# Keys copied and norm products made behind a filling step, attention's filling in a fixed period, and a gate block's weight sums made one block earlier, in a hybrid attention and recurrence block

## The chip, the cores and the metric

The kernel runs on one core of a Trainium2 chip. The engines are TensorE (PE: matmuls, PEld: its weight loads), VectorE (DVE), ScalarE (ACT), GpSimd (POOL) and SyncE (SP), whose queue issues most loads. The metric is the time of one execution on the device in microseconds, as the median of several runs. The profile is of one further execution, recorded by the hardware profiler.

## The reference

One layer works on 1024 tokens of width 1024 in float32: a normalisation, one wide input projection, two branches in parallel, gates that merge them, an output projection, and an MLP with a squared ReLU. Cut to what the change touches:

```python
u = rmsnorm(x, norm1_g) @ w_in          # q, k, v of attention; f, i, q, g of the recurrence; two gates
# attention, 8 heads of 64: weights by a running product over the keys
w = where(mask, exp(log_beta + between), 0);  o_sb = w @ v
# HGRN2, 4 heads of 128: S_t = diag(f_t) S_{t-1} + k_t v_t^T, o_t = S_t^T q_t
o_hg = hgrn2_chunkwise(silu(q_hg), k_hg, i_hg, log_f)
o_hg = rmsnorm(o_hg, hg_norm_g) * silu(g_hg)
merged = sigmoid(gate_sb + b0) * (o_sb @ w_o_sb) + sigmoid(gate_hg + b1) * (o_hg @ w_o_hg)
h = x + merged @ w_out
```

Every product in float32 is made of three matmuls on a high and a low half of both operands (`three`), so each operand is first split: a copy on ACT makes the high half (L157), a subtraction on DVE the low half (L162). Large projections (gates, output, MLP) use sums of blocks in place of some products, so that weights and inputs are also added before they are split.

## The kernel before

**What sets the order.** The program is written as one list of instructions, and a planner that runs when the kernel is built gives each engine its own order: by what it estimates to be ready, and among ready ones the instruction written first. It also deals out tiles. `slot` gives one of 40 full tiles of 128 x 1024, `half` and `slot_n` (up to 512 columns) one of 10 half tiles, `bank` one of 8 PSUM banks, and weights on their way use two buffers each of `raw`, `whi` and `wlo`; a tile that isn't free is waited for. On the chip each engine then follows its own order and waits at semaphores. Where the author wants an order, `after(ins, earlier)` puts one instruction behind another on the same engine; `load` (L136) chains all loads on SP in the order in which they are written.

**Filling.** PE's order has two lanes. "main" blocks are those with a chain of work on other engines between them: scores and turned weights of attention, levels and tails of the recurrence. "fill" blocks are projections, which need nothing of that chain. `Stream` (L504) holds the filling as a list of jobs, each a generator; `st.advance(n, upto)` takes n steps of it, but not past job `upto`. A step of a projection is six matmuls of 512 columns. A projection job has nine steps: the fifth also evicts the first half, the ninth has no matmul and only evicts the second. The first step of a job also splits the weights of the next and starts the load of the one after (`prefetch`).

**Attention** (L2610 to L2648). 64 items, eight blocks of 128 queries for each of eight heads, in the order 7, 0, 6, 1, 5, 2, 4, 3. Item i writes the running product of item i+1 (`weights`, a scan on DVE), the scores of item i+2 (`scores`), its share of filling steps, then the turn of its own weights by PE with their split (`turn`: tiles wTh and wTl), then the value product (`values`: tile po) of the last pair of blocks that is complete. So values run behind blocks 1, 5 and 3 and, in the middle of its turn, behind block 7. The shares of filling come from `n_fill`, spread evenly over the 64 items.

**The recurrence** (L2651 to L2671). For each of four heads `hg_levels` has a first part and seven levels. Level l > 0 copies the keys that it needs into a half tile (`scores_of`, L1096 to L1099, ACT, tile ksl), multiplies them with the queries on PE (tile sl), lays the scores into place, then multiplies keys, queries and decays on DVE for the next level. `hg_tail` of the head before turns keys, sums states, and makes the output: matmuls into two banks (pho), squares with their sums on ACT (hon), a root on POOL (`inv_rms`, L266 and L270), the product of bank and root on DVE (L1281, into hon), and two rounds later transposes. After each `yield` of the one or the other, the loop takes `FILL[h]` filling steps on average (2.0 to 3.4).

**The gate blocks** (`GatePair` and `gates`, L1767 to L1983). Ten blocks, the first two of them (8 and 9) for the branch's own gate, the third is block 0. `load` fetches three blocks of weights and, for the others than 8 and 9, the output weights; `load_sums` fetches partial results; `split` adds weight blocks three times and splits what comes out; then follow products x6, y5, x7, y3 into two banks, gX and gY. In `gates`, while block v is made, `next_pair` splits block n, the one behind it, and loads block m, the one behind that. The first block is loaded and split earlier, in `sum_forms` (L1562), which runs beside the filling and whose last parts run just before `gates`. `held` are gate products whose last steps wait for this stage; they fill in between.

## Time and profile before

| | |
|---|---|
| median of 3 runs | 1428.94 us (1428.68 to 1429.35) |
| profiled execution | 1427.22 us |
| its span, first to last instruction | 1425.4 us |
| mean granted TensorE clock | 0.998 |
| busy share: PE, DVE, ACT, POOL | 99%, 75%, 47%, 12% |

The profiled execution's own time is 1.8 us above its span and 1.7 us below the median. In rows of the order of time the columns are: start in us from the span's start, duration in us, engine, line of the kernel, operation, output<-inputs, shapes, count, and in brackets the engine's idle time before it and what ended it. Names leave out numbers of buffers, so that ksl is the copy of the keys of any head and level. Rows of waits are: who waited, for whom, total us, how often, longest. A line such as L129 is that of a helper; the tiles tell which part of the kernel it is.

### The profile page before, as it was taken

To read this page: it belongs to the slowest core of one execution; us is meant where nothing else is said; L and a number is where in the kernel's file an instruction comes from. 1 tells how busy PE (TensorE), PEld (TensorE's weight loads), DVE (VectorE), ACT (ScalarE), POOL (GpSimd) and SP (SyncE) were. 2 spreads that over 40 slices of the span, in tenths; PEclk is the share of its full clock that TensorE was granted. 3 is DMA by queue.
4 is the path that set the end of the run, shared out by engine and by line. 5 is a ranking of instruction groups with operands and counts; after the bars stand their busy time and mean duration, and the time that the engine had idled before them with its cause. 6 is when DMAs were issued, how large, how long until landed. Compare 5 with 4: busy or idle time off the path is not lost.

```text
span 1425.4 us, 18660 instructions
## 1 busy us (share of the span) xinstructions
PE 1406.0 (99%) x6824; PEld 1179.2 (83%) x6824; DVE 1066.6 (75%) x1463; ACT 668.1 (47%) x1147; POOL 166.4 (12%) x318
## 2 busy tenths in 40 slices
PE   9999999999999999999999999999999999999997
PEld 8888888888887888788888888888888888888886
DVE  6688887778478858897788897677666657768765
ACT  6455556554245446433334764445444443433343
POOL 3023433310001111000000300000000000000042
PEclk9999999999999999999999999999999999999999
DMA  8256977954213676464485515444446974776724
GB/s 252 82 141 200 173 157 170 228 127 123 87 52 104 207 228 230 162 214 155 153 290 207 185 39 183 162 158 138 142 146 236 356 264 152 275 280 237 277 98 172
DMA packets 169556, 258.18 MB, mean 181 GB/s; under 512 B 31404, under 2 KB 92376, under 8 KB 169432
## 3 DMA queue, kind: packets, MB, share of 16 engines
q1 hardware_dynamic: 148280, 196.15, 40.9%
q0 software_dynamic: 16320, 50.34, 13.8%
q10 hardware_dynamic: 4864, 10.49, 2.1%
q8 instruction: 54, 0.88, 0.3%
q14 instruction: 38, 0.31, 0.1%
HBM read 186.69 MB, written 84.94 MB: 191 GB/s over the span
## 4 chain that ended last, share of the span: by engine, by line
PE 91%; DVE 4%; ACT 2%; DMA 1%; issue 1%; POOL 0%; SPq 0%; ACTq 0%; POOLq 0%; DVEq 0%
PE pm L129 21%; PE pX L129 9%; PE pW L129 6%; PE pY L129 6%; PE pjqk L129 6%; PE gY L129 3%; PE pji L129 3%; PE pga L129 3%; PE pyh L129 3%; PE gX L129 3%; PE pjq L129 3%; PE pjf L129 3%; PE po L129 3%; PE pwX L129 2%; PE pjv L129 2%; PE z L129 2%
## 5 line engine op out<-in xcount | busy, mean ns | idle before, releaser
L859 DVE TENSOR_TENSOR_SCAN rm<-rm,bits 128x512 f32<-128x512 f32 (+6 forms) x72 | 87.6, 1222 | 26.7 <-ACT rm L840 24.3
L157 ACT CAST whid<-w 128x1024 fp32r<-128x1024 f32 x30 | 31.6, 1054 | 154.3 <-PE pm L129 86.9
L129 PE MATMUL pm<-wlod,sh 128*128 128x512 f32 x240 | 93.5, 390 | 0.0
L129 PE MATMUL pm<-whid,sh 128*128 128x512 f32 x240 | 93.4, 389 | 0.0
L129 PE MATMUL pm<-whid,sl 128*128 128x512 f32 x240 | 93.4, 389 | 0.0
L129 PE MATMUL pm<-tl,sh 128*128 128x512 f32 (+1 forms) x210 | 81.3, 387 | 0.0
L129 PE MATMUL pm<-th,sl 128*128 128x512 f32 (+1 forms) x210 | 81.3, 387 | 0.0
L129 PE MATMUL pm<-th,sh 128*128 128x512 f32 (+1 forms) x210 | 81.3, 387 | 0.0
L162 DVE TENSOR_TENSOR wlod<-w,whid 128x1024 fp32r<-128x1024 f32 x30 | 36.6, 1221 | 55.1 <-ACT whid L157 55.0
L157 ACT CAST wTh<-pw 128x128 fp32r<-128x128 f32 (+3 forms) x96 | 43.8, 481 | 56.3 <-PE pw L132 51.6
L2387 POOL TENSOR_SCALAR fss<-fss 128x1 f32<-128x1 f32 x8 | 4.5, 561 | 562.0 <-ACT fsc L2382 561.5
L162 DVE TENSOR_TENSOR sl<-sa,sh 128x1024 fp32r<-128x1024 f32 x56 | 68.2, 1218 | 0.4 <-ACT sh L157 0.4
L162 DVE TENSOR_TENSOR wTl<-pw,wTh 128x512 fp32r<-128x512 f32 (+2 forms) x96 | 50.4, 546 | 22.5 <-ACT wTh L157 21.0
L157 ACT CAST sh<-sa 128x1024 fp32r<-128x1024 f32 x56 | 57.2, 1046 | 8.2 <-DMA sa<-ad 8.2
L129 PEld LDWEIGHTS pm<-wlod,sh 128*128 128x128 f32 x240 | 45.0, 188 | 9.8 <-DVE wlod L162 0.4
L129 PEld LDWEIGHTS pm<-whid,sh 128*128 128x128 f32 x240 | 45.1, 188 | 9.3
L129 PEld LDWEIGHTS pm<-whid,sl 128*128 128x128 f32 x240 | 45.0, 188 | 9.4
L129 PE MATMUL pX<-sqh,t1l 128*128 128x512 f32 x128 | 49.9, 390 | 0.0
L129 PE MATMUL pX<-sql,t1h 128*128 128x512 f32 x128 | 49.9, 390 | 0.0
L129 PE MATMUL pX<-sqh,t1h 128*128 128x512 f32 x128 | 49.8, 389 | 0.0
L129 PEld LDWEIGHTS pm<-tl,sh 128*128 128x128 f32 x210 | 39.5, 188 | 8.1
L129 PEld LDWEIGHTS pm<-th,sl 128*128 128x128 f32 x210 | 39.5, 188 | 8.0
(985 smaller groups left out, 4414.8 us busy)
## 6 DMA issues: line engine op xcount, KB each, us to landing
w<-in_w_ff_dram SPq DMA_DIRECT2D x72, 512.0 KB, 5.7
sa<-ad SPq DMA_DIRECT2D x52, 512.0 KB, 6.7
tg<-in_w_in_dram POOLq DMA_DIRECT2D x16, 512.0 KB, 9.5
ad<-a SPq DMA_DIRECT2D x32, 256.0 KB, 4.5
ad<-s SPq DMA_DIRECT2D x16, 512.0 KB, 3.3
tw<-in_w_out_dram POOLq DMA_DIRECT2D x24, 256.0 KB, 5.8
pr<-pd SPq DMA_DIRECT2D x10, 512.0 KB
x<-in_x_dram SPq DMA_DIRECT2D x8, 512.0 KB, 10.5
```

What stands on the lines that cost most here:

```text
L129: return pe(nc.tensor.matmul(*a, **k))
L157: hi_last[0] = after(in_turn("act", nc.scalar.copy(dst, src)), hi_behind[0])
L162: nc.vector.tensor_tensor(out=dst, in0=src, in1=hi.bitcast(F32), op=ALU.subtract),
L859: sc = nc.vector.tensor_tensor_scan(out=rr, data0=rr, data1=bits[:, 1024 - nk + a : 1024 - nk + b][:, ::-1], initial=rm[:, b : b + 1] if i ...
L2387: nc.gpsimd.tensor_scalar(out=ssq, in0=ssq, scalar1=1.0 / D, scalar2=EPS, op0=ALU.mult, op1=ALU.add)
```

## The change

- `keys_of` is split off `scores_of`. Level l puts the copy of level l+1's keys into a list, `soon`, and the loop of the recurrence now takes its filling steps one by one and empties the list after each. So the copy is written behind the first filling step of level l instead of behind all of them.
- The product of bank and root in `hg_tail` goes into the same list.
- In attention `n_fill` is 116 instead of 111 and the share 14 steps for each head of eight items, always 1, 2, 2, 2, 1, 2, 2, 2 (before, the pattern shifted from head to head); filling may run into the job behind, q of head 2.
- The third gate block's weights are loaded in the last part of `sum_forms`, into two full tiles of their own, and its three adds (`sums`) stand where its load was, in the first block's `next_pair`. Its `split` leaves them out.

```diff
+    soon = []
+
     def hg_levels(h):
...
+        ahead = {}
+
+        def keys_of(name, H):
+            ahead[name] = slot_n(f"k{name}", 512)
+            nc.scalar.copy(
+                ahead[name].rearrange("p (n s h) -> p s n h", s=2, h=H), crossed(k, 0, H)
+            )
+
         def scores_of(name, H):
-            keys = slot_n(f"k{name}", 512)
-            nc.scalar.copy(
-                keys.rearrange("p (n s h) -> p s n h", s=2, h=H), crossed(k, 0, H)
-            )
+            keys = ahead.pop(name)
             open_block("main")
...
             hg_level[0] = mul(right, right, left)
+            if l < 6:
+                soon.append(lambda l=l, H=H: keys_of(f"sl{h}_{l + 1}", 2 * H))
...
             rstd = inv_rms(ssq, 4, 1.0 / P, f"hn{h}_{half}")
-            mul(chunks(on), chunks(po), rstd.unsqueeze(2).to_broadcast([P, 4, P]))
+            soon.append(
+                lambda on=on, po=po, rstd=rstd: mul(
+                    chunks(on), chunks(po), rstd.unsqueeze(2).to_broadcast([P, 4, P])
+                )
+            )
...
             if i == 3:
                 gates_in[0].load_sums()
                 gates_in[0].split()
+            if i == 7:
+                gates_in[2].load()
             yield
...
-                if self is gates_in[0]
+                if self in (gates_in[0], gates_in[2])
...
+        def sums(self):
+            r0, r1 = self.raw
+            s0, s1 = slice(0, 512), slice(512, 1024)
+            add(r0[:, s0], r0[:, s1], r0[:, s0])
+            add(r1[:, s0], r1[:, s1], r0[:, s0])
+            add(r0[:, s1], r1[:, s1], r0[:, s1])
...
-            after(add(r0[:, s0], r0[:, s1], r0[:, s0]), first)
-            add(r1[:, s0], r1[:, s1], r0[:, s0])
+            if self is not gates_in[2]:
+                after(add(r0[:, s0], r0[:, s1], r0[:, s0]), first)
+                add(r1[:, s0], r1[:, s1], r0[:, s0])
...
-            add(r0[:, s1], r1[:, s1], r0[:, s1])
+            if self is not gates_in[2]:
+                add(r0[:, s1], r1[:, s1], r0[:, s1])
...
-        if m:
+        if m is gates_in[2]:
+            m.sums()
+        elif m:
             m.load()
...
-    n_fill = 9 * (NHS - 1 + 5) + 3
     n_first = 4
+    n_fill = n_first + 14 * NHS
...
-        st.advance(want - done, j_att)
+        st.advance(want - done, j_q[2])
...
-                    st.advance(int(owed), upto)
+                    for step in range(int(owed)):
+                        st.advance(1, upto)
+                        while soon:
+                            soon.pop(0)()
                     owed -= int(owed)
```

## The prediction

> **What bounds the kernel.** I read the page first, then busy time by stretches, then the waits of the matmul engine, then the order of time around each of its waits.

> ```profile
> PE 1406.0 (99%) x6824; PEld 1179.2 (83%) x6824; DVE 1066.6 (75%) x1463; ACT 668.1 (47%) x1147; POOL 166.4 (12%) x318
> ```

> TensorE (PE) is busy for 1406.0 us, 99% of the span. The change adds and removes no matmul, so it can only win PE's idle time, and only where it reaches. The next view has one row per stage: projections (to 85), attention (to 318), the gated recurrence with its filling (to 560), the first gate blocks (to 600), the rest.

> ```profile
> core 0: us, PE busy (x) PEld busy (x) DVE busy (x) ACT busy (x) POOL busy (x), PEclk, DMA share, GB/s
> 0.00:85.00 85.00, 82.03 (x419) 69.56 (x420) 55.75 (x115) 45.04 (x91) 17.02 (x40) 1.00 0.56 166
> 85.00:318.00 233.00, 230.18 (x1331) 198.89 (x1330) 188.41 (x238) 134.25 (x308) 74.38 (x156) 1.00 0.76 172
> 318.00:560.00 242.00, 237.84 (x1258) 201.59 (x1258) 176.84 (x306) 109.57 (x239) 25.73 (x42) 1.00 0.44 144
> 560.00:600.00 40.00, 38.49 (x170) 31.58 (x169) 33.98 (x47) 18.14 (x24) 2.59 (x5) 1.00 0.61 205
> 600.00:1110.00 510.00, 510.00 (x2294) 423.26 (x2293) 395.79 (x537) 238.64 (x339) 22.47 (x43) 1.00 0.50 172
> ```

> PE idles 2.82 us in attention, 4.16 in the recurrence, 1.51 in the first gate blocks, and not at all from 600 to 1110. The sum, 8.5 us, is all that lies in the change's reach. Who ends these waits, from 85 to 600:

> ```profile
> PE sl L129 <- ACT ksl L1097: 3.6, 3, 2.0
> PE po L129 <- DVE wTl L162: 2.7, 4, 1.0
> PE gY L129 <- DVE pr L1324: 1.5, 1, 1.5
> PE pga L129 <- DVE wga7wlo L162: 0.5, 1, 0.5
> PE po L129 <- ACT wTh L157: 0.2, 1, 0.2
> ```

> Ten waits, each with a part of the change aimed at it: level scores (sl) wait for the copy of the keys (ksl, `keys_of`), the attention's value products (po) for the low half of the turned weights (wTl), gate block gY for a subtraction, a filling step for the low half of its weights.

> A wait costs slightly more than its idle time, since the modelled ends of matmuls overlap the next start:

> ```profile
> 209.55 0.40 PE L129 MATMUL pjqk<-xnh,wqk6h 128*128 128x512 f32 x1
> 209.78 0.40 PE L129 MATMUL pjqk<-xnl,wqk6h 128*128 128x512 f32 x1
> 211.02 0.39 PE L129 MATMUL po<-wTl,V 128*128 128x256 f32 x1 [0.84 <-DVE wTl L162]
> ```

> Starts stand 0.23 us apart where nothing waits, and 1.24 here: 1.01 lost for 0.84 idle. I add these 0.17 us to each wait. The prices are then: keys 3.56 + 3 x 0.17 = 4.1 us; attention 2.82 + 5 x 0.17 = 3.7; gY 1.7; wga7wlo 0.7. Together 10.2 us.

> **The keys' copies.** Before, the copy of level l+1 is written behind all filling steps of level l; after, behind the first one. The same 24 copies run; none is added.

> ```profile
> 514.98 0.69 ACT L1290 ACTIVATE on<-pot,prm 128x512 f32<-128x512 f32 x1 [3.39 <-PE pot L132]
> 516.38 0.69 ACT L1460 ACTIVATE g<-pga,prm 128x512 f32<-128x512 f32 x1 [0.71 <-PE pga L129]
> 516.96 0.61 ACT L1097 COPY ksl<-k 128x512 f32<-128x512 f32 x1
> ```

> ```profile
> 510.65 0.69 DVE L170 TENSOR_TENSOR k<-k,pp 128x512 f32<-128x512 f32 x1
> ```

> ```profile
> 515.94 0.40 PE L129 MATMUL pga<-xnh,wga1wlo 128*128 128x512 f32 x1
> 517.62 0.38 PE L129 MATMUL sl<-q,ksl 128*128 128x128 f32 x1 [1.28 <-ACT ksl L1097]
> ```

> The keys are final at 510.65 + 0.69 = 511.34, and ACT then stands idle for 3.39 us; yet the copy comes last, behind two evictions that wait for PE, the second being of the filling step written just ahead of it. Copied where they are ready, the keys would be there at 512, and PE would go on at 516.2. The largest wait, 1.96 us at 448.88, has the same form; its product and its copy:

> ```profile
> 439.48 0.68 DVE L170 TENSOR_TENSOR k<-k,pp 128x512 f32<-128x512 f32 x1
> ```

> ```profile
> 448.20 0.62 ACT L1097 COPY ksl<-k 128x512 f32<-128x512 f32 x1
> ```

> What is late next is the queries' product, which VectorE (DVE) does right behind the keys' and as fast (0.7 us), in both places well before PE asks. So I take the whole 4.1 us. Bounds: 0 (the copies keep their place in ACT's order, which the build's planner sets) and 4.1; the loss is a rival below. A copied tile lives longer by one or two filling steps and takes one of ten half tiles; I price that among the new waits.

> ```profile
> L1097 ACT COPY ksl<-k x24: 607/622/698, 324.5 to 529.0; 128x512 f32<-128x512 f32 x24
> ...
> DVE k L170: 20.9, 8
> ```

> ACT already waits in front of key copies, 20.9 us in 8 waits, and what stands behind them waits too: a queue in its written order. [...]

> **The norm products.** Eight products (hon) move behind the first filling step after their squares.

> ```profile
> 551.67 0.69 DVE L170 TENSOR_TENSOR hon<-pho,hn_y 128x512 f32<-128x512 f32 x1 [1.18 <-POOL hn_y L270]
> 552.27 0.68 DVE L162 TENSOR_TENSOR wga7wlo<-wga7r,wga7whi 128x512 fp32r<-128x512 f32 x1
> ```

> This one waits 1.18 us for POOL's root, the low half of wga7 stands behind it, and PE waits for that (0.7 us). Put behind, the product would let wga7wlo go first. Whether it does is the planner's estimate of POOL against ACT, which no row shows: between 0 and 0.7, I take half, 0.35. The other seven hide beside PE's work; their readers, the transposes, come two filling rounds later. The norm's bank stays open for one filling step more.

> **The attention.** Filling rises from 111 to 116 steps, and each head gets the same 1, 2, 2, 2, 1, 2, 2, 2 over its eight blocks (7, 0, 6, 1, 5, 2, 4, 3). A step of six matmuls is 1.36 us (six starts 0.23 apart); five more of them here are five fewer later, so they cost nothing as such. I counted both lists: before, every wait above 0.5 us falls on a value product right behind a block in which a job ends and the next starts, or one without a matmul of filling. One of them on DVE:

> ```profile
> 164.83 1.20 DVE L1522 TENSOR_TENSOR xs<-xs,xnl 128x1024 f32<-128x1024 f32 x1
> 166.06 0.70 DVE L162 TENSOR_TENSOR KS<-pjqk,KS 64x512 fp32r<-64x512 f32 x1
> 166.77 0.68 DVE L162 TENSOR_TENSOR QL<-pjqk,QH 64x512 fp32r<-64x512 f32 x1
> 167.38 1.21 DVE L162 TENSOR_TENSOR wqk5l<-wqk5r,wqk5h 128x1024 fp32r<-128x1024 f32 x1
> 168.51 0.68 DVE L162 TENSOR_TENSOR wTl<-pw,wTh 128x512 fp32r<-128x512 f32 x1
> ```

> The job's end (KS, QL), the next weights (wqk5l) and an input sum stand ahead of wTl, 3.8 us. In the new list this bundle sits right ahead of a value product in two places: head 2, block 4 (the same bundle, one block earlier, but with 12 matmuls of filling behind it instead of 6: I take 0.9) and head 7, block 6 (no input sums left: 0.1). Head 1, block 7 keeps one step behind a job's end: 0.4. The block without filling moves to head 4, block 7, where its value product follows 3 us later, enough for 1.4 us of copy and subtraction: 0. Small ones 0.3. So 1.7 us come back and 2.0 are won; bounds 3.7 won and, with the single step now ahead of the values in all seven later heads and 1.0 for each, 7.0 - 3.7 = 3.3 lost.

> **The gate block.** The third block's three adds move from 577 to 586 into the first block's time, its four loads ahead of the held gates' loads on SP's queue.

> ```profile
> 576.50 0.69 DVE L1324 TENSOR_TENSOR gu<-gY,gu 128x512 f32<-128x512 f32 x1 [1.44 <-PE gY L129]
> ...
> 586.00 0.68 DVE L1321 TENSOR_TENSOR wg0r<-wg0r,wg0r 128x512 f32<-128x512 f32 x1
> ...
> 589.47 0.68 DVE L1324 TENSOR_TENSOR pr<-gY,pr 128x512 f32<-128x512 f32 x1
> ```

> PE waits until 590.21 for that last subtraction; its matmul before started at 588.31, so it could have gone on at 588.54. The row of 576.50 is the last with idle time; from there DVE's rows follow without a gap, with the three adds (577.71, 584.26, 586.00) among them. An add holds DVE for 0.6 us (from 586.00 to the next start at 586.60), so without them the subtraction ends 1.8 us earlier, at 588.36, and the wait goes, by 0.2 us. I take 1.7, bounds 0 and 1.7. The adds' new place is the stretch from 565 to 574, in which DVE has most of its idle 6.0 us of the row 560 to 600; if their loads land later, DVE stands before the adds, and bounds for that are 0 and those 6.0 us; I take 0. On SP's queue the loads now pass those of the held gates:

> ```profile
> 558.00 0.96 SPq L137 DMA_DIRECT2D y<-yd  x2
> ```

> ```profile
> 577.11 0.68 DVE L170 TENSOR_TENSOR g<-g,y 128x512 f32<-128x512 f32 x1
> ```

> Their reader comes 19 us later, which covers four more issues and a wait for the two further full tiles that the third block's weights now take from the pool.

> **New waits and the sum.** Earlier copies, later products and a filling that runs one step ahead reorder every engine from 90 to 600. Ten waits of 1.0 us on average stand there now; I take two new ones, 2.0 us (bounds 0 and 6). Sum: -4.1 - 0.35 - 2.0 - 1.7 + 2.0 = -6.1 us. The profiled execution took 1427.22 us, 1.7 below the median of the runs, 1428.94; the same 6.1 us off each gives 1421.1 and, for the median, **1422.8 us**.

> **Rivals.** (a) *The attention's waits only move.* For: a single step now precedes values in every head, and blocks in which a job ends still drift. Against: the three largest of before had the bundle ahead of them. Without the 2.0 us: 1424.8. (b) *The copies and products stay where they were*, as the planner sends what it deems ready: the change doesn't do what it says. For: in heads 0 and 1 ACT already waits for k, so copies run as early as they can there. Against: at 511 an idle ACT did not take a copy that was ready. Without 4.1 and 0.35, and with one new wait: -2.0 - 1.7 + 1.0 = -2.7, 1426.2. (c) *Slower: copies ahead of evictions.* In heads 2 and 3, twelve copies now stand before evictions of the filling. If one waits for its keys the mean of the 8 waits, 20.9 / 8 = 2.6 us, and PE needs the bank behind it, PE stands. Four such add 10.4 us: -6.1 + 10.4 = +4.3, 1433.2; from four on it is slower than before by more than a measurement can tell. Against: none of the 8 held PE.

> **Chances.** Forecast 0.47, (a) 0.20, (b) 0.18, (c) 0.12, and 0.03 that all ten waits go (1428.94 - 10.2 = 1418.7). A measurement of this kernel can tell about 0.2%, 2.9 us. The forecast is faster but for 0.04, (a) in three of four, (b) in two of five: faster 0.68, same 0.19, slower 0.13. The range 1419.5 to 1428.5 holds the forecast, (a) and (b), and leaves out (c) and the last case.

> **What would show it.** Right: no idle row at sl behind ksl from 430 to 520, with copies within 1 us of their k product; hon behind wga7wlo; gY without a wait and wg0r adds near 570; the largest remaining po wait in head 2. Wrong: copies still behind evictions (b); pga, pys or p evictions waiting behind ksl (c); po waits in most heads at block 7 (a); DVE idle before wg0r.

## The result and the profile after

| | median of runs (lowest to highest) | ratio to before, 95% interval |
|---|---|---|
| before | 1429.14 us (1428.68 to 1430.27) | |
| after | 1420.33 us (1418.52 to 1421.75) | 0.9936 [0.9919, 0.9954] |
| before, second set | 1428.26 us (1426.94 to 1428.96) | |
| after, second set | 1420.94 us (1418.93 to 1421.28) | 0.9948 [0.9936, 0.9961] |

The change wins 8.8 us in the first set and 7.3 in the second, against 6.1 forecast. The profiled execution of after took 1421.75 us, with a span of 1420.0 (before: 1427.22 and 1425.4). Busy time by stretches, first three columns PE, PEld and DVE as before:

```profile
core 0: us, PE busy (x) PEld busy (x) DVE busy (x) ACT busy (x) POOL busy (x), PEclk, DMA share, GB/s
85.00:318.00 233.00, 230.01 (x1315) 198.88 (x1314) 185.32 (x234) 130.52 (x300) 74.86 (x159) 0.99 0.76 172
318.00:560.00 242.00, 241.97 (x1291) 206.50 (x1290) 182.45 (x314) 116.33 (x249) 26.25 (x42) 1.00 0.46 149
560.00:600.00 40.00, 40.00 (x179) 33.10 (x178) 36.66 (x52) 16.81 (x22) 2.17 (x4) 1.00 0.54 176
```

PE's idle time in the recurrence fell from 4.16 us to 0.03 and in the first gate blocks from 1.51 to nothing. In attention it did not fall at all: 2.82 before, 2.99 after. And the PEclk column, which was 1.00 in every row of before, is 0.99 there. PE's waits of after, from 85 to 600:

```profile
PE po L129 <- DVE wTl L162: 2.3, 2, 2.2
PE pjq L129 <- ACT osb L934: 0.4, 1, 0.4
PE z L129 <- ACT rm L840: 0.2, 1, 0.2
```

All ten old waits are gone; nearly all that is left is one wait of 2.17 us. It ends at 171.18, at head 2, block 3, with DVE as the engine that is late:

```profile
165.62 1.22 DVE L1535 TENSOR_TENSOR xs<-xs,xnl 128x1024 f32<-128x1024 f32 x1
166.75 1.22 DVE L859 TENSOR_TENSOR_SCAN rm<-rm,bits 128x512 f32<-128x512 f32 x1
168.00 0.70 DVE L162 TENSOR_TENSOR KS<-pjqk,KS 64x512 fp32r<-64x512 f32 x1
168.72 0.68 DVE L162 TENSOR_TENSOR QL<-pjqk,QH 64x512 fp32r<-64x512 f32 x1
169.32 1.21 DVE L162 TENSOR_TENSOR wqk5l<-wqk5r,wqk5h 128x1024 fp32r<-128x1024 f32 x1
170.46 0.87 DVE L162 TENSOR_TENSOR wTl<-pw,wTh 128x512 fp32r<-128x512 f32 x2
```

```profile
168.07 0.60 PE L132 MATMUL pw<-ident,rm 128*128 128x128 f32 x4
168.42 0.36 PE L129 MATMUL po<-wTh,V 128*128 128x256 f32 x1
168.62 0.40 PE L129 MATMUL pjq<-xnh,wq0h 128*128 128x512 f32 x1
171.18 0.39 PE L129 MATMUL po<-wTl,V 128*128 128x256 f32 x1 [2.17 <-DVE wTl L162]
...
171.64 0.28 PE L129 MATMUL po<-wTh,V 128*128 128x256 f32 x1
171.76 0.31 PE L129 MATMUL po<-wTl,V 128*128 128x256 f32 x1
171.88 0.40 PE L129 MATMUL po<-wTh,V 128*128 128x256 f32 x1
172.09 0.42 PE L129 MATMUL po<-wTl,V 128*128 128x256 f32 x1
172.30 0.41 PE L129 MATMUL po<-wTh,V 128*128 128x256 f32 x1
```

DVE has no gap from 165.62 to wTl. Behind the wait the value products start 0.12 us apart up to 171.88, and from there 0.21 apart: PE's clock has halved. The stretches around it, in after:

```profile
168.47:171.88 3.41, 1.24 (x9) 0.92 (x8) 3.40 (x6) 0.59 (x1) 0.79 (x2) 1.00 0.83 136
171.88:175.30 3.42, 3.42 (x14) 3.13 (x13) 2.69 (x4) 1.64 (x4) 1.36 (x2) 0.50 0.81 190
175.30:178.71 3.41, 3.41 (x25) 3.09 (x25) 2.66 (x2) 1.65 (x6) 0.19 (x2) 1.00 0.89 185
```

The granted clock is 0.50 for 3.41 us, then full again. Half of 3.41, so by estimate 1.7 us, is lost behind the wait, and no idle row shows it.

**Does it add up?** I took each matmul's distance from the start of the one before, subtracted the usual (median) distance of matmuls of its kind, and added up all excess over 0.06 us from 85 to 620. That is 21.6 us before and 16.0 after; the difference, 5.6, is the difference of the two spans (5.4). In attention the excess rose from 9.8 to 11.0; behind it, it fell from 11.7 to 5.0.

### The profile page after: what moved, and what is told of

It reads as the page before. It is cut to its first block, busy times and chain, and to the rows that moved or that the text cites. A ratio compares the mean times of both kernels' runs of the same rounds, so it can differ in the third digit from the quotient of the medians.

```text
span 1420.0 us, 18679 instructions
## 1 busy us (share of the span) xinstructions
PE 1406.0 (99%) x6824; PEld 1181.1 (83%) x6824; DVE 1066.9 (75%) x1463; ACT 667.8 (47%) x1147; POOL 164.4 (12%) x318
## 4 chain that ended last, share of the span: by engine, by line
PE 95%; DVE 1%; ACT 1%; DMA 1%; issue 1%; SPq 0%; POOL 0%; POOLq 0%; DVEq 0%
PE pm L129 21%; PE pX L129 9%; PE pW L129 6%; PE pY L129 6%; PE pjqk L129 5%; PE gY L129 4%; PE gX L129 4%; PE pga L129 4%; PE pjf L129 3%; PE pji L129 3%; PE pyh L129 3%; PE pjq L129 3%; PE pys L129 3%; PE po L129 3%; PE pwX L129 2%; PE z L129 2%
## 5 line engine op out<-in xcount | busy, mean ns | idle before, releaser
L157 ACT CAST whid<-w 128x1024 fp32r<-128x1024 f32 x30 | 31.6, 1054 | 154.1 <-PE pm L129 83.2
L129 PE MATMUL pm<-whid,sh 128*128 128x512 f32 x240 | 93.4, 389 | 0.0
L129 PE MATMUL pm<-wlod,sh 128*128 128x512 f32 x240 | 93.4, 389 | 0.0
L129 PE MATMUL pm<-whid,sl 128*128 128x512 f32 x240 | 93.4, 389 | 0.0
L129 PE MATMUL pm<-tl,sh 128*128 128x512 f32 (+1 forms) x210 | 81.3, 387 | 0.0
L129 PE MATMUL pm<-th,sl 128*128 128x512 f32 (+1 forms) x210 | 81.3, 387 | 0.0
L129 PE MATMUL pm<-th,sh 128*128 128x512 f32 (+1 forms) x210 | 81.3, 387 | 0.0
L162 DVE TENSOR_TENSOR wlod<-w,whid 128x1024 fp32r<-128x1024 f32 x30 | 36.7, 1223 | 53.6 <-ACT whid L157 53.6
L157 ACT CAST wTh<-pw 128x512 fp32r<-128x512 f32 (+2 forms) x96 | 43.8, 483 | 57.9 <-PE pw L132 54.2
L162 DVE TENSOR_TENSOR sl<-sa,sh 128x1024 fp32r<-128x1024 f32 x56 | 68.3, 1219 | 0.4 <-ACT sh L157 0.3
L162 DVE TENSOR_TENSOR wTl<-pw,wTh 128x512 fp32r<-128x512 f32 (+2 forms) x96 | 50.4, 546 | 21.8 <-ACT wTh L157 20.7
L157 ACT CAST sh<-sa 128x1024 fp32r<-128x1024 f32 x56 | 57.2, 1046 | 9.0 <-DMA sa<-ad 9.0
L129 PEld LDWEIGHTS pm<-wlod,sh 128*128 128x128 f32 x240 | 45.1, 188 | 9.5
L129 PEld LDWEIGHTS pm<-whid,sl 128*128 128x128 f32 x240 | 45.1, 188 | 9.3
L129 PEld LDWEIGHTS pm<-whid,sh 128*128 128x128 f32 x240 | 45.0, 187 | 9.4
L129 PE MATMUL pX<-sqh,t1l 128*128 128x512 f32 x128 | 49.9, 390 | 0.0
L129 PE MATMUL pX<-sql,t1h 128*128 128x512 f32 x128 | 49.9, 390 | 0.0
L129 PE MATMUL pX<-sqh,t1h 128*128 128x512 f32 x128 | 49.8, 389 | 0.0
L840 ACT ACTIVATE rm<-z 128x512 f32<-128x512 f32 (+3 forms) x96 | 44.5, 501 | 8.4 <-DMA sx<-xs 5.7
L129 PEld LDWEIGHTS pm<-th,sh 128*128 128x128 f32 x210 | 39.5, 188 | 8.1
```

Of the source, the lines that this page charges most:

```text
L129: return pe(nc.tensor.matmul(*a, **k))
L157: hi_last[0] = after(in_turn("act", nc.scalar.copy(dst, src)), hi_behind[0])
L162: nc.vector.tensor_tensor(out=dst, in0=src, in1=hi.bitcast(F32), op=ALU.subtract),
L840: scored[0] = nc.scalar.activation(rm[:, s0 : s0 + m], z[:, :m], AF.Sigmoid, scale=-0.125)
```

## The experiments

My theory was that each part removes the waits it is aimed at, and that they add. The rival was that the whole filling, moved by one step, did the recurrence's share too. Every part was first made alone in the kernel before; the median of before beside these four was 1427.71 us.

**The keys' copies alone.**

```diff
-            keys = slot_n(f"k{name}", 512)      # in scores_of
-            nc.scalar.copy(...)
+            keys = ahead.pop(name)
...
+            if l < 6:
+                soon.append(lambda l=l, H=H: keys_of(f"sl{h}_{l + 1}", 2 * H))
```

> Before with the keys' copies alone moved behind the first filling step. Theory 1 (each part removes its own waits): the three waits of sl for ksl between 430 and 520 us are gone, 4.1 us less (about 1425.0), all other waits of before stand unchanged. Theory 2 (the waits went because the filling runs one step further ahead in the recurrence): at least two of the three waits are still there, the time within 1 us of before. Theory 3 (early copies hold back evictions behind them): the waits for ksl are gone but new ones for evictions stand in their place, the gain under 2 us.

1422.22 us, ratio 0.996 [0.9947, 0.9972]: 5.5 us less than the median of before. The three waits for ksl are gone, every other wait of before is still there:

```profile
PE po L129 <- DVE wTl L162: 2.6, 4, 1.0
PE gY L129 <- DVE pr L1333: 1.5, 1, 1.5
PE pga L129 <- DVE wga7wlo L162: 0.5, 1, 0.5
PE po L129 <- ACT wTh L157: 0.2, 1, 0.2
```

The copy for the scores that waited at 517.62, with what follows it on ACT, and the scores on PE:

```profile
508.11 0.62 ACT L1101 COPY ksl<-k 128x512 f32<-128x512 f32 x1
511.59 0.69 ACT L1299 ACTIVATE on<-pot,prm 128x512 f32<-128x512 f32 x1 [2.86 <-PE pot L132]
512.98 0.69 ACT L1469 ACTIVATE g<-pga,prm 128x512 f32<-128x512 f32 x1 [0.70 <-PE pga L129]
```

```profile
512.55 0.39 PE L129 MATMUL pga<-xnh,wga1wlo 128*128 128x512 f32 x1
512.78 1.05 PE L129 MATMUL sl<-q,ksl 128*128 128x128 f32 x8
```

It now stands ahead of the two evictions that held it, is done at 508.73, and the scores start 0.23 us behind the matmul before them. Theory 1 holds; the gain is somewhat above the 4.1 that idle time and restart give. By the excess of starts it is 5.0 from 270 to 560: after each wait the second matmul was 0.1 us late too, and a delay of 0.3 us at wga0wlo (483.29) went as well. The 0.5 us above that come from before: 12 of its 27 executions have a mean granted clock of 0.997 and took 1428.86 us on average, the other 15, at 0.998 or 0.999, took 1427.26. Against these 15 the five of this kernel (0.998 or 0.999, mean 1422.20) gain 5.1. The last section says where the two groups come from.

**The norm products alone.**

```diff
-            mul(chunks(on), chunks(po), rstd...)
+            soon.append(lambda on=on, po=po, rstd=rstd: mul(chunks(on), chunks(po), rstd...))
```

> Before with the eight norm products alone moved behind the first filling step after their squares. Theory 1: the low half of wga7 goes ahead of the product that waits for POOL's root, PE's wait of 0.5 us near 553 is gone, 0.7 us less (about 1428.4). Theory 2: that wait stands or another takes its place, no change. The difference is at the edge of what the timing can tell; the trace decides.

1427.35 us, ratio 0.9999 [0.999, 1.0008]: nothing. (Its eight executions at 0.998 or 0.999 took 1427.24 us on average, those of before 1427.26.) On DVE the product is still ahead of the low half of wga7 and still waits for POOL:

```profile
551.89 0.69 DVE L170 TENSOR_TENSOR hon<-pho,hn_y 128x512 f32<-128x512 f32 x1 [1.18 <-POOL hn_y L270]
552.50 0.68 DVE L162 TENSOR_TENSOR wga7wlo<-wga7r,wga7whi 128x512 fp32r<-128x512 f32 x1
```

Written later, it kept its place. Why the planner put it there, the trace does not show.

**The attention's filling alone.**

```diff
-    n_fill = 9 * (NHS - 1 + 5) + 3
     n_first = 4
+    n_fill = n_first + 14 * NHS
...
-        st.advance(want - done, j_att)
+        st.advance(want - done, j_q[2])
```

> Before with the attention's fixed filling period alone (116 instead of 111 steps). Theory 1: the five waits of po of before go (3.7 us) and the waits seen after the whole change stand here too, the largest, some 2.2 us, near 171 at head 2, block 3; a net gain between 0 and 1.5 us, less by up to 1.7 us where PE's granted clock halves behind that wait. The three waits for ksl in the recurrence are still there, moved or not. Theory 2: with the filling one step ahead, the waits for ksl near 449, 462 and 517 are gone without any change to the copies, and the gain is over 4 us.

1426.75 us, ratio 0.9991 [0.9982, 1.0]. PE's waits:

```profile
PE sl L129 <- ACT ksl L1097: 4.0, 4, 1.5
PE po L129 <- DVE wTl L162: 2.3, 2, 2.2
PE gY L129 <- DVE pr L1324: 1.1, 1, 1.1
PE pjq L129 <- ACT osb L934: 0.2, 1, 0.2
```

The waits for ksl are now four, and with 4.0 us in sum no shorter than the three of before (3.6): the rival, theory 2, falls. The five attention waits are gone and the 2.17 us wait stands in their place. The wait for wga7wlo is gone here, with the norm products where they were: it was this part that removed it.

**The gate block's sums alone.**

```diff
+            if i == 7:
+                gates_in[2].load()
...
-        if m:
+        if m is gates_in[2]:
+            m.sums()
+        elif m:
             m.load()
```

> Before with the third gate block's loads and sums alone moved into the first gate block. Theory 1: the wait of gY for the subtraction (1.5 us near 590) is gone and the sums stand between 560 and 580, 1.7 us less (about 1427.2). Theory 2: DVE stands before the sums for their loads and PE waits for something else there: gain under 0.5 us.

1426.6 us, ratio 0.9989 [0.9981, 0.9998]: 1.1 us less. The second and third sum wait 0.30 us for their load and hold up nobody; gY does not wait any more.

```profile
572.55 1.29 DVE L1321 TENSOR_TENSOR wg0r<-wg0r,wg0r 128x512 f32<-128x512 f32 x2 [0.30 <-DMA wg0r<-in_w_in_dram]
```

This profiled execution has a halved clock (below), so the 1.5 us of idle time that went is not seen in full in its time.

Alone the four give 5.5 + 0.4 + 1.0 + 1.1 = 8.0 us, the whole 7.3 to 8.8: as far as these medians can tell, the parts add. Next, three of the parts were taken out of the changed kernel (before beside them: 1428.92 us).

**Without the keys' copies.**

```diff
-            keys = ahead.pop(name)
+            keys = slot_n(f"k{name}", 512)
+            nc.scalar.copy(...)
```

> The changed kernel with the keys' copies written back behind all filling steps. By the copies alone the time was 5.5 us shorter; if that holds beside the other parts, this kernel is about 5 us slower than the changed one, near 1424.5, with three or four waits of sl for ksl (some 4 us) back in the recurrence. If the filling's shift by one step would have removed these waits anyway, it stays within 1.5 us of the changed kernel.

1424.49 us, ratio 0.9971 [0.9959, 0.9982], 3.6 to 4.2 above the two medians of after, with four waits for ksl of 4.0 us in sum. As expected.

**Without the norm products' move.**

```diff
-            soon.append(lambda on=on, po=po, rstd=rstd: mul(...))
+            mul(chunks(on), chunks(po), rstd...)
```

> The changed kernel with the norm products written back where they were. If the products did nothing, as alone, the time is that of the changed kernel within 0.7 us and no wait for wga7wlo appears near 551 (the shifted filling removed it). If they matter beside the other parts, that wait of 0.5 us is back and the time 0.7 us longer.

1420.04 us, ratio 0.9941 [0.9929, 0.9954]: the time of after, with no wait for wga7wlo. This part of the change does nothing here.

**Without the attention's filling.**

```diff
+    n_fill = 9 * (NHS - 1 + 5) + 3
     n_first = 4
-    n_fill = n_first + 14 * NHS
...
-        st.advance(want - done, j_q[2])
+        st.advance(want - done, j_att)
```

> The changed kernel with the attention's filling as before (111 steps, the old spread). The parts alone gave 5.5 (keys), 0.4 (norm products) and 1.1 us (gate); their sum gives about 1420.7, the same as the whole change within a microsecond. The five old waits of po for wTl (2.8 us) are back, the wait of 2.2 us at head 2, block 3 is not there, and the runs lie within 1 us of each other, as those of the keys alone did, since no PE wait reaches 1.9 us. Rival: without the shifted filling new waits appear in the recurrence, and the time is over 1423.

1421.0 us, ratio 0.9948 [0.9935, 0.996], runs from 1420.47 to 1421.29. As expected: as it stands, the new period is worth about nothing beside the other parts. The five attention waits of before are back, and so is the one for wga7wlo (0.5 us), although the norm products are moved in this kernel: they do not remove it.

**The low half of wqk5 behind the turned weights.** The input sum, the scan, KS, QL and wqk5l fill DVE ahead of wTl at 170.46. If that bundle is the cause, taking from it must shorten the wait.

```diff
-                if self.name in ("wf1", "wqk6") or self.name == "wv" and i == 1:
+                if self.name in ("wf1", "wqk6", "wqk5") or self.name == "wv" and i == 1:
```

> The changed kernel with the low half of wqk5 written behind the subtraction of the turned weights instead of ahead of it. If that low half (1.21 us on DVE) is what makes the value product of head 2, block 3 late, its wait falls from 2.17 to about 1.0 us, and the granted clock no longer halves behind it in any run: 1.2 us less in every execution and up to 1.7 less where the clock fell, median near 1418, spread under 1.5 us. If the wait is ended by something else, the time is that of the changed kernel. If the halved clock has nothing to do with the wait, it is still there in some runs and the spread stays near 3 us.

1418.65 us (1417.85 to 1419.33), ratio 0.993 [0.9918, 0.9943]. The wait is 1.30 us, not 1.0, and no clock falls behind it (1.00 from 169.54 to 172.95). On the same chip the kernel without the norm products' move, whose wait is the 2.17 us of the changed kernel, took 1420.04: 1.4 us more.

Three runs followed on one chip (before beside them: 1428.26 us). First the changed kernel once more:

> The changed kernel once more, beside the next two on the same chip. Median 1419 to 1421.5; if the halved clock behind the wait of 2.2 us comes only in some executions, its runs fall in two groups about 1.5 us apart, and those with the lower granted clock are the longer ones.

1420.94 us; its profiled execution has the halved clock again, 0.50 from 170.29. The two groups were not clean: 1418.93, then 1420.73 to 1421.28.

**The bundle made longer.**

```diff
-                after(after(hi_lo(h, l, r), last_lo[0]), attended[0])
+                first = after(after(hi_lo(h, l, r), last_lo[0]), attended[0]); again[0] = after(lo_sub(l, r, h), first) if self.name == "wqk5" else again[0]
...
-            turn_hi[0] = hi_last[0]
+            after(turn_lo[0], again[0]); turn_hi[0] = hi_last[0]
```

> The changed kernel with the low half of wqk5 subtracted twice, both ahead of the turned weights' subtraction of head 2, block 3 (one more instruction of 1.2 us on DVE, the same result). The wait of po there grows from 2.2 to some 3.5 us. If a longer wait makes the halved clock likelier, every run shows it: the granted clock 0.997 or less and the time 1.3 us (the wait) plus up to 1.7 us (the clock) above the changed kernel, some 1422 to 1423. If the clock falls for a reason other than the wait, its share of runs stays as it was and the time grows by 1.3 us alone.

1420.44 us, not 1422 to 1423. The wait grew to 2.47 us only: PE did five more filling matmuls ahead of it, work that it would otherwise have had to do later. The clock fell in the profiled execution (0.50 from 172.12); in how many others, only their mean granted clocks hint (0.997 in three of five, not in all). This run didn't tell what it was meant to.

**Two input sums moved on as well.** Beside the wqk5 edit:

```diff
-        if i > 2 and i % 5 > 1:
+        if (i > 2 and i % 5 > 1 and i not in (22, 23)) or i in (25, 26):
             next(insums, None)
```

> The kernel with wqk5's low half behind the turned weights, and two input sums of 1.2 us each moved three items later, away from head 2, block 3. The remaining wait there (1.3 us) should shrink by up to 1.2 us, as one sum stood ahead of KS and QL on DVE: median near 1417.6, 1 us less than with the low half moved alone. Rival: the sums or their stores are late for their next reader, or KS waits for its matmuls rather than for the sum: no gain, or a new wait near 180.

1417.88 us (1416.67 to 1419.19), ratio to before 0.9931 [0.9917, 0.9944], and 3.1 us below the changed kernel on the same chip. It is the lowest median, but against the before beside each it gains 10.4 us and the wqk5 edit alone 10.3: what moving the two sums adds, these times cannot tell. In the trace it shows. PE's only wait from 85 to 600, and DVE in the disputed place:

```profile
PE po L129 <- DVE wTl L162: 0.2, 1, 0.2
```

```profile
165.32 0.69 DVE L162 TENSOR_TENSOR KS<-pjqk,KS 64x512 fp32r<-64x512 f32 x1
166.02 0.68 DVE L162 TENSOR_TENSOR QL<-pjqk,QH 64x512 fp32r<-64x512 f32 x1
166.63 0.87 DVE L162 TENSOR_TENSOR wTl<-pw,wTh 128x512 fp32r<-128x512 f32 x2
167.43 1.21 DVE L162 TENSOR_TENSOR wqk5l<-wqk5r,wqk5h 128x1024 fp32r<-128x1024 f32 x1
```

wTl follows QL at once, and the sum and wqk5l hide behind it. The span is 1414.8 us, 10.6 less than before, and the excess of starts, 11.2, is 10.4 less.

## Why the prediction was right, and where it was not

The forecast of the time was near, but two of its terms were wrong, each by about 2 us, and cancelled each other. That part of the agreement is luck.

| step | forecast | in the traces | alone, timed |
|---|---|---|---|
| keys' copies | -4.1 | three waits gone: -4.1; all starts: -5.0 | -5.5 (-5.1, clock at 0.998 and up) |
| norm products | -0.35 | 0 | -0.4, interval around 0 |
| attention's filling | -2.0 | 3.7 won, 3.8 back; wga7wlo, 0.7, won | -1.0 |
| gate's sums | -1.7 | wait gone: -1.7 | -1.1 |
| new waits elsewhere | +2.0 | none | |

- **The keys** were right in cause and, within 1 us, in size: the copy was late by its place in ACT's queue, and early it leads by 4 us. Rival (b) falls. Rival (c) did see something real: ACT now waits for k longer than the 20.9 us of before,

```profile
ACT ksl L1101 <- DVE k L170: 33.4, 13, 7.6
```

  but none of these 33.4 us reached PE.
- **The attention** is the step that failed. I had named the place (the bundle at head 2, from 0.9 us) and the first heads' small waits, but three things were mis-sized. I priced only the bundle of before, 3.8 us, while a scan of 1.22 us now stands in it, so that DVE is busy for 4.84 us from 165.62 to 170.46. I counted twelve matmuls of filling as cover, but all of them stand ahead of the turn (pw at 168.07); between the turn and the waiting product is a single one, at 168.62. And I had no price for the halved clock. So 3.8 us came back (idle 2.99, and 0.17 for each of five waits) instead of 1.7, and rival (a), that attention's waits only move, is what happened to this term.
- **New waits** were put at 2.0 us beside those. The recurrence and the gates have none: with the copies early and the sums away, PE had work there all the time (idle 0.03 us from 318 to 560, and 0 from 560 to 600).
- **The norm products** did not move (my lower bound). The wait that they were to remove went by the filling's shift, which I hadn't seen.
- **The gate block** was right: the sums stand at 566 to 569 in after, and the wait is gone.

The sum of the trace's terms is -4.1 - 1.7 - 0.7 + 0.1 = -6.4, and the halved clock gives 1.7 back in the profiled execution. That leaves 4.7, where the two profiled executions differ by 5.5. The 0.8 between them would be covered by delays too short to be listed as waits, such as the 0.9 us that the keys won beyond their 4.1; I did not split it further. The medians fell by more than 6.1 because before, by its granted clock (0.997 in 23 of the 47 executions of the last section), loses time behind its longest wait as well, in about half of its executions, and both medians of before in the first table are as long as those executions (1428.26 and up).

## What to carry to other kernels

Where an engine is idle and a ready operation stands behind ones that are not, look at where it was written: moving one copy ahead of two evictions gave most of this gain (alone 5.5 us, of 7.3 to 8.8). Cover for a chain counts only from where the chain starts: filling ahead of the transposes did not hide the copy and the subtraction behind them (twelve matmuls stood ahead of pw at 168.07, and PE still waited 2.17 us). When filling is spread anew, list for each place what meets on the engine behind it; here one edit, which put a subtraction of 1.2 us on DVE behind that of the turned weights, made some 2 us of a spread that had been worth nothing (1418.65 us, against 1421.0 with the old spread). And where executions of one kernel fall into groups, compare group with group: a median moves with their shares (those of before lie 1.6 us apart).

## What the hardware showed

| trace | longest wait, us | most idle in one stretch | clock halved behind it |
|---|---|---|---|
| wqk5_twice | 2.47 | 2.47 | yes |
| after, after_again | 2.17 | 2.17 | yes |
| gate_alone | 1.96 | 1.96 | yes |
| no_keys | 2.18 | 1.84 | yes |
| before, norm_alone | 1.96 | 1.51 | no |
| attention_alone | 2.17 | 1.49 | no |
| no_norm | 2.17 | 1.47 | no |
| wqk5_late | 1.30 | 1.30 | no |
| keys_alone | 1.51 | 1.07 | no |
| no_attention, late_sums | 0.96, 0.29 | 0.96, 0.29 | no |

The same wait of 1.96 us at 449, once within one stretch and once across two. In gate_alone:

```profile
446.33:449.75 3.42, 1.46 (x12) 1.04 (x10) 1.75 (x3) 2.38 (x6) 1.20 (x2) 1.00 0.00 0
449.75:453.16 3.41, 3.41 (x10) 2.69 (x9) 2.81 (x7) 1.66 (x3) 0.00 (x0) 0.50 0.40 154
```

In norm_alone:

```profile
445.06:448.47 3.41, 2.06 (x13) 1.47 (x11) 1.74 (x4) 2.63 (x11) 1.20 (x2) 1.00 0.33 128
448.47:451.88 3.41, 2.80 (x16) 2.50 (x17) 3.41 (x7) 1.59 (x4) 0.00 (x0) 1.00 0.10 23
```

1.96 us idle in one stretch: the next runs at half the clock (0.50). 1.35 and 0.61 in two: the clock stays at 1.00. From that wait to the next one in the list (517.62 in before, 519.12 in gate_alone) gate_alone takes 70.36 us and before 68.74, so the halved clock cost 1.6. By the table the limit lies between 1.51 and 1.84 us of idle time in a stretch of 3.41. The end of keys_alone narrows it: its last matmul ends at 1412.27, so in the stretch from 1410.66 to 1414.08 PE is idle for 1.81 us, and the clock stays full all through the next, until 1417.49 (the mean granted clock of this execution is 0.999). By this count the limit is above 1.81, so not quite at half a stretch (1.71); but the ends of matmuls are modelled, and what exactly is counted, these runs do not settle.

This explains why executions of before spread over 2.6 us beside the four parts alone (1426.76 to 1429.38) and those of keys_alone, whose longest wait is 1.51, over 1.0. Only one execution of each kernel was traced, but the mean granted clock of every execution is known to three digits. Before was executed 47 times beside the experiments: the 23 executions at 0.997 took 1428.26 to 1430.14 us, the 24 at 0.998 or 0.999 took 1426.76 to 1427.76. Beside the four parts alone the two groups' means are 1.6 us apart, the price of one halved stretch. And none of the 20 executions of the four kernels without a wait above 1.51 us (keys_alone, no_attention, wqk5_late, late_sums) has 0.997, while each of the others has it in some. In a single execution it is no sure sign: after_again and no_keys have 0.998 in the profiled execution, with a halved stretch in its trace. Nor is the halved clock the only cause of spread: late_sums, without any long wait, spread over 2.5 us, and why is open. A wait long enough to pass the limit wherever the grid lies was not tried.
